# Inverting the 16x16 diagonal blocks of a triangular system by substitution on the vector engine, in a hybrid decoder layer

## The chip, the cores and the metric

The kernel runs on one core of a Trainium2 chip. Its engines are called as the profile calls them: PE is the matrix engine (PEld its weight load), DVE the vector engine (VectorE), ACT the scalar engine (ScalarE), POOL is GpSimd, SP the engine that only issues transfers. Each executes its own instructions in order; they wait for each other through semaphores. The metric is the device time of one execution in microseconds, median over runs.

## The reference

One layer of a decoder for a prompt of 256 tokens and eight samples of four tokens, model width 2048, float32. Three branches work on the same normalised input: a gated short convolution (A), a gated DeltaNet (B, 8 heads of 128) and a chunked gating MLP (C). Gates merge them, an output projection and a gated ConvFFN follow. The change touches branch B of the prompt:

```python
kb = kc * bc[..., None]
lmat = jnp.where(strict, jnp.einsum('nbhcd,nbhed->nbhce', kb, kc) * decay, 0.0)
eye = jnp.eye(C, dtype=jnp.float32)
tmat = lax.linalg.triangular_solve(eye + lmat, jnp.broadcast_to(eye, lmat.shape),
                                   left_side=True, lower=True, unit_diagonal=True)
u = jnp.einsum('nbhce,nbhef->nbhcf', tmat, vb)
w = jnp.einsum('nbhce,nbhed->nbhcd', tmat, kb * jnp.exp(gcum)[..., None])
```

For every head and every chunk of tokens a unit lower triangular matrix I + L is inverted. The result does not depend on the chunk length; the kernel takes chunks of 128 tokens, so it inverts 16 matrices of 128x128 (8 heads, 2 chunks).

## The kernel before

**The stream.** All large weights come as 614 tiles of 128 x 8 x 128 (`raw`, 512 KB, four buffers, issued from SP). ACT rounds a tile to `wh` (L74), DVE forms the remainder `wl = raw - wh` (L81), each with three buffers, and PE multiplies the eight 128x128 blocks of the tile with the 288 token columns in three passes: wh times the activations' high part (L202), wh times their low part (L203), wl times the high part (L204). A unit of 16 or 8 such blocks accumulates in one `acc` bank of PSUM and is then evacuated. One tile of the stream, 24 matmuls, is called a slot here. At the start of a slot `Stream.next` emits, in this order: one background step, outstanding `wl`, the load of the tile five ahead, `wh` and `wl` of the tile two ahead, and the evacuations that were put off.

**The background.** Everything else that needs PE between units is written as a generator, `delta()`, whose `yield`s cut it into steps; `pump` takes one step at the start of a slot. Beside the units for q, k and v it takes one step in every second slot: when a unit of these has just ended, `heavy` skips the step. The order of every engine's queue is the order in which the code emits. So a step's instruction that waits holds up what that engine was given later: on DVE the next `wl`, on PE the next slot's matmuls.

**The solve.** `delta()` goes through four groups g of two heads, four matrices (head, chunk) each, tiles [128, 4, 128]. It normalises k, forms k k^T and k q^T (L750, L751), scales k k^T into L in place (`dec`, four L119), and inverts by doubling: at level s the blocks of size s on the diagonal are joined in pairs. `T` holds the inverse so far and `U` its transpose; `B` is L times a mask m_s that leaves the squares to be eliminated at this level. At s=1 one product with the identity (L761) turns B; then for s = 2, 4, ..., 64, in two steps:

- first step: PE forms four products w of B and U (L771), ACT copies them to `W`, POOL masks the next B (L778);
- second step: PE forms four products of T and W (L782) and four of W and T (L784), DVE subtracts them from U and T.

One correction (L790, L799) and the rest of the recurrence follow. In the profile `bank` is a PSUM bank of the background and `mall` holds the masks; `U1`, `vn`, `on`, `sq` are tiles [128, 4, 128] that later parts use. Of the four groups, g=0 runs beside the q, k, v units (about 190 to 350 us), g=1 and g=2 beside the gate and output units of branch C, and g=2's end and g=3 beside branch A, whose units have a short convolution.

Of the kernel before, what the change touches and what calls it, by code (L numbers as in the profile page):

```python
# [6 lines left out]
F32 = mybir.dt.float32  # L7
F32R = mybir.dt.float32r
AF = mybir.ActivationFunctionType
ALU = mybir.AluOpType  # L10
AX = mybir.AxisListType

P = 128
# [19 lines left out]

V_LNI, V_LN1, V_LN2, V_CA, V_CB, V_CF, V_NB = 0, 32, 64, 96, 120, 216, 345
V_N = 346
MK = ("tri", "mbT", "mbS", "m1", "m2", "m4", "m8", "m16", "m32", "m64",
      "tri4", "ones4", "mbT4", "mbS4", "ones")
SM_HM, SM_BM, SM_N = 0, 4, 12

# [59 lines left out]
def body(tc, I, O):  # L99
    nc = tc.nc  # L100
    V, A, G, PE = nc.vector, nc.scalar, nc.gpsimd, nc.tensor
    top = ExitStack()

    def pool(stack, name, bufs=1, psum=False):
        if psum:
            return stack.enter_context(tc.tile_pool(name=name, bufs=bufs, space=bass.MemoryType.PSUM))
        return stack.enter_context(tc.tile_pool(name=name, bufs=bufs))

    def copy(out, in_, scale=None):
        if scale is None:  # L110
            A.activation(out=out, in_=in_, func=AF.Copy)  # L111
        else:
            A.activation(out=out, in_=in_, func=AF.Identity, scale=scale)

    def tt(out, a, b, op):
        V.tensor_tensor(out=out, in0=a, in1=b, op=op)  # L116

    def stt(out, a, s, b, op0, op1):
        V.scalar_tensor_tensor(out=out, in0=a, scalar=s, in1=b, op0=op0, op1=op1)  # L119
# [13 lines left out]
    def mid(ap, n):  # L133
        return ap.unsqueeze(1).to_broadcast([ap.shape[0], n, ap.shape[1]])
# [8 lines left out]
    tmp = pool(top, "tmp", 2)  # L143
# [5 lines left out]
    def bank():  # L149
        return bgp.tile([P, 512], F32, name="bank", tag="bank")  # L150
# [82 lines left out]
    ident = const.tile([P, P], F32, name="ident")  # L233
# [142 lines left out]
        copy(e[:, r:r + NTP], a[:, 0:NTP])  # L376
        copy(es[:, :, r:r + LS], samp(a[:, NTP:NT]))

    # ---------------------------------------------------------------- input norm
    mstack = ExitStack()  # L380
    Mp = pool(mstack, "Mp")
    M = Mp.tile([P, KD, NT], F32, name="M")
# [10 lines left out]
    for j in range(2):  # L393
        s = BLK[j][0]
# [27 lines left out]
    st.subs()  # L422
    st.dma(4)

    # ---------------------------------------------------------------- branch C
    wsT = cp.tile([P, H, P], F32, name="wsT")
    wsS = cp.tile([NTS, H, NTS], F32, name="wsS")
    bsr = cp.tile([P, H, P], F32, name="bsr")
# [1 line left out]
    tri = cp.tile([P, P], F32, name="trim")  # L430
# [8 lines left out]
    G.dma_start(out=gbr, in_=I["lnc"])  # L439
    G.dma_start(out=tri, in_=I["masks"][:, 1 + MK.index("tri"), :])  # L440
    G.dma_start(out=tri4, in_=I["masks"][0:NTS, 1 + MK.index("tri4"), 0:NTS])
    G.dma_start(out=wsT, in_=I["wsT"])
# [91 lines left out]
    flush()  # L534
    cstack.close()

    # ---------------------------------------------------------------- branches A, B
    astack = ExitStack()
    ap = pool(astack, "ap")
    QF = ap.tile([P, H, NTP], F32, name="QF")  # L540
# [99 lines left out]
    def delta():  # L640
        ds = ExitStack()
        mp = pool(ds, "dmask")
        mk = {}
        mall = mp.tile([P, len(MK), P], F32, name="mall")
        G.dma_start(out=mall, in_=I["masks"][:, 1:1 + len(MK), :])
        for i, n in enumerate(MK):
            mk[n] = mall[:, i, :]
# [6 lines left out]
        KF, VF = (kvp.tile([P, H, NTP], F32, name=n) for n in ("KF", "VF"))  # L654
        QKV.extend((KF, VF))
        ddp = ds.enter_context(tc.tile_pool(name="ddp", bufs=1, space=bass.MemoryType.DRAM))
        identR = mp.tile([P, P], F32R, name="identR")
        copy(identR, ident)
        yield
        ps = bank()  # L660
        gp = bg_g[:, 0:2, 8:16]
# [3 lines left out]
        f = lambda i: dtok[:, i].rearrange("p c h -> p (c h)")  # L665
# [16 lines left out]
        def D(tag, dt=F32, n=4):  # L682
            return dp.tile([P, n, P], dt, name=tag, tag=tag)

        def b4(bk):
            return bk[:, :].rearrange("p (u t) -> p u t", t=P)

        I4 = mid(ident, 4)
# [11 lines left out]
        for g in range(4):  # L700
# [20 lines left out]
            sq = D("sq")  # L721
# [9 lines left out]
            dT = D("decT")  # L731
# [16 lines left out]
            kk, kq = b4(bank()), b4(bank())  # L748
# [3 lines left out]
            for u in range(4):  # L752
                hh, c = divmod(u, 2)
                stt(Dm[:, u, :], kk[:, u, :], bg_g[:, c, 2 * g + hh:2 * g + hh + 1], Dm[:, u, :], ALU.mult, ALU.mult)
            L = Dm
            B = D("B", F32R)
            tt(B, L, mid(mk["m1"], 4), ALU.mult)
            yield
            w = b4(bank())
            for u in range(4):  # L760
                PE.matmul(w[:, u, :], lhsT=B[:, u, :], rhs=identR, start=True, stop=True)  # L761
            U, T = D("U", F32R), D("T", F32R)
            tt(T, I4, B.bitcast(F32), ALU.subtract)
            tt(U, I4, w, ALU.subtract)
            B = D("B", F32R)
            G.tensor_tensor(out=B, in0=L, in1=mid(mk["m2"], 4), op=ALU.mult)
            yield
            for s in (2, 4, 8, 16, 32, 64):
                w = b4(bank())
                for u in range(4):  # L770
                    PE.matmul(w[:, u, :], lhsT=B[:, u, :], rhs=U[:, u, :], start=True, stop=True)  # L771
                W = D("W", F32R)
                copy(W, w)
                if s == 2:
                    tt(dT, kq, dT, ALU.mult)
                if s < 64:
                    B = D("B", F32R)
                    G.tensor_tensor(out=B, in0=L, in1=mid(mk["m%d" % (2 * s)], 4), op=ALU.mult)  # L778
                yield
                pu, pt = b4(bank()), b4(bank())  # L780
                for u in range(4):
                    PE.matmul(pu[:, u, :], lhsT=T[:, u, :], rhs=W[:, u, :], start=True, stop=True)  # L782
                for u in range(4):
                    PE.matmul(pt[:, u, :], lhsT=W[:, u, :], rhs=T[:, u, :], start=True, stop=True)  # L784
                tt(U, U.bitcast(F32), pu, ALU.subtract)
                tt(T, T.bitcast(F32), pt, ALU.subtract)
                yield
            w = b4(bank())
            for u in range(4):
                PE.matmul(w[:, u, :], lhsT=L[:, u, :], rhs=U[:, u, :].bitcast(F32), start=True, stop=True)  # L790
            F0, F = D("sq"), D("W", F32R)
# [5 lines left out]
            w = b4(bank())  # L797
            for u in range(4):
                PE.matmul(w[:, u, :], lhsT=T[:, u, :], rhs=F[:, u, :], start=True, stop=True)  # L799
            U1 = D("U1")  # L800
            tt(U1, U.bitcast(F32), w, ALU.add)
            yield
            vn, on = D("vn"), D("on")
            S = D("S", n=2)
            for c in range(2):
                us = (c, 2 + c)
                if c:
                    w = b4(bank())
# [8 lines left out]
                w = b4(bank())  # L817
# [4 lines left out]
                w = b4(bank())  # L822
# [15 lines left out]
            sq = D("sq")  # L838
# [20 lines left out]
        mp = pool(ds, "smask")  # L859
# [34 lines left out]
        def E(tag, n=1):  # L894
            return dp.tile([P, n * P], F32, name=tag, tag=tag)

        for p in range(2):
# [4 lines left out]
            Dm, dT = E("sdec"), E("sdecT")  # L902
# [9 lines left out]
            sq = E("ssq", 2)  # L912
# [22 lines left out]
            B = E("sB")  # L935
# [5 lines left out]
            for hl in range(4):  # L941
                for b in range(NB):
                    PE.matmul(kso[:, :, hl, b, :], lhsT=stt_[4 * p + hl][:, b, :], rhs=KQv[:, :, hl, b, :], start=True, stop=True)  # L943
                if hl == 0:
                    w = bank()
                    PE.transpose(w[:, 0:P], B, ident)
                    U, T, B2 = E("sU"), E("sT"), E("sB2")
# [3 lines left out]
                if hl == 1:  # L951
                    w = bank()
# [3 lines left out]
                if hl == 2:  # L956
                    w = bank()
# [7 lines left out]
            w = bank()  # L965
            for i in range(2):
                PE.transpose(w[:, i * P:(i + 1) * P], KS[:, i * P:(i + 1) * P], ident)
            on = E("son")
# [3 lines left out]
            w = bank()  # L972
            PE.matmul(w[:, 0:P], lhsT=U, rhs=R, start=True, stop=True)
            copy(kv[:, P:2 * P], w[:, 0:P])
            vn = kv[:, P:2 * P]
# [6 lines left out]
            w = bank()  # L982
# [52 lines left out]
        ds.close()  # L1035

    background[0] = delta()
    next(background[0])

# [94 lines left out]
        unit("win", (C_G + 2048, m), X, KD, gate_evac(gs))  # L1134
        unit("wb", m, YB, H, out_b(m))

    # ---------------------------------------------------------------- output projection, LN1
    l1stack = ExitStack()
    l1p = pool(l1stack, "l1p")
    Y = l1p.tile([P, KD, NT], F32, name="Y")  # L1140
# [147 lines left out]
            chain[m]()  # L1288
    flush()

    # ---------------------------------------------------------------- gated embedding, ConvFFN
    def pg_evac(m):
        def e(a):
            s = held()
            A.activation(out=s, in_=a[:, 0:NT], func=AF.Sigmoid)

            def fin():
                tt(M[:, m, :], M[:, m, :], s, ALU.mult)
                t = short()
                tt(t, XH[:, m, :].bitcast(F32), XL[:, m, :].bitcast(F32), ALU.add)  # L1300
                stt(M[:, m, :], t, ALPHA, M[:, m, :], ALU.mult, ALU.add)
            staged.append(fin)
        return e
# [48 lines left out]
    for half, nf in enumerate(FH):  # L1352
        for i in range(nf):
            f = f0 + i
# [11 lines left out]
    op = pool(fstack, "op")  # L1366
# [36 lines left out]
def _masks(np):  # L1403
    i = np.arange(P)
    r, c = i[:, None], i[None, :]
    blk = (r // 4) == (c // 4)
    f = np.float32
    m = [(r == c).astype(f), (r <= c).astype(f),
         np.where(c >= r, f(0), f(-BIG)).astype(f), np.where(r > c, f(0), f(BIG)).astype(f)]
    for s in (1, 2, 4, 8, 16, 32, 64):  # L1410
        m.append((((r // (2 * s)) == (c // (2 * s))) & ((r // s) % 2 == 1) & ((c // s) % 2 == 0)).astype(f))
    m += [((r <= c) & blk).astype(f), blk.astype(f),
          np.where((c >= r) & blk, f(0), f(-BIG)).astype(f), np.where((r > c) & blk, f(0), f(BIG)).astype(f),
          np.ones((P, P), f)]
    return np.ascontiguousarray(np.stack(m, 1))
# [88 lines left out]
```

## Time and profile before

| | us |
|---|---|
| median of 3 runs | 2128.73 |
| lowest and highest run | 2127.16, 2128.85 |
| span of the profiled execution | 2130.0 |
| PE busy | 2118.1 |
| DVE busy | 1201.7 |
| ACT busy | 963.9 |
| POOL busy | 240.6 |

The profiled execution is known by its span, from its first to its last instruction, 2130.0 us; it lies 1.3 us above the median of the runs. Busy shares are means over stages. In rows of the chain of waits and of the timeline the first number is the start in the span, the second the duration, both in us; a bracket gives the idle time ahead of the instruction on its engine and what ended it. In rows of groups stand the busy time in us, the mean of one in ns, and the idle time before. In rows of DMA issues the last number is the median time from issue to landing in us. In rows of windows stand, after the length, busy time and count for PE, PEld, DVE, ACT and POOL, then the granted clock of PE as a share of full speed, the DMA share and GB/s.

### The profile page before, as it was taken

Reading aid. Unit: us, or ns where it says so; the run is one execution under the profiler, and the core shown is the slowest. Engines: PE = TensorE matmul, PEld = TensorE weight load, DVE = VectorE, ACT = ScalarE, POOL = GpSimd, SP = SyncE. Lnnn points to the kernel's source line nnn. Section 1 sums busy time; section 2 is a strip of 40 time slices with the busy share of each in tenths; the row PEclk is TensorE's granted clock in tenths of the full one; section 3 lists DMA queues with packets and bytes.
Section 4 is the critical chain, followed back from the end, with each engine's and each line's share of the span. In section 5 each row is a group of like instructions: output and inputs, shape, how many; then the busy total and the mean of one; then the engine's idle time right before and its main releaser. Section 6 shows DMA issues by size and latency. Waiting matters only on the chain.

```text
span 2130.0 us, 38253 instructions
## 1 busy us (share of the span) xinstructions
PE 2118.1 (99%) x15866; PEld 2095.6 (98%) x15866; DVE 1201.7 (56%) x1640; ACT 963.9 (45%) x1484; POOL 240.6 (11%) x447
## 2 busy tenths in 40 slices
PE   9999999999999999999999999999999999999999
PEld 7999999999999999999999999999999999999997
DVE  5657765555665556555577755555544455555444
ACT  6447554343434445443344634444433344444333
POOL 1112320101111212000000201111100011111000
PEclk9999999999999999999999999999999999999998
DMA  6444444443435456444544444444444444444442
GB/s 232 146 160 155 158 154 147 141 145 138 147 138 188 144 212 215 163 168 163 184 166 143 154 168 165 162 168 162 165 168 163 164 168 161 167 166 169 162 157 93
DMA packets 95998, 345.66 MB, mean 162 GB/s; under 512 B 11072, under 2 KB 11632, under 8 KB 95664
## 3 DMA queue, kind: packets, MB, share of 16 engines
q1 hardware_dynamic: 92352, 331.11, 44.5%
q0 software_dynamic: 3472, 12.11, 1.8%
q8 instruction: 124, 2.03, 0.4%
q14 instruction: 50, 0.41, 0.1%
HBM read 334.90 MB, written 8.28 MB: 161 GB/s over the span
## 4 chain that ended last, share of the span: by engine, by line
PE 98%; DVE 1%; ACT 0%; DMA 0%; issue 0%; POOL 0%; POOLq 0%; SPq 0%; DVEq 0%; ACTq 0%
PE acc L202 31%; PE acc L204 31%; PE acc L203 30%; PE bank L310 1%; PE bank L943 1%; PE bank L784 1%; PE bank L782 0%; PE bank L771 0%; PE bank L276 0%; DMA yt<-in_x 0%; PE bank L718 0%; DVE lnst L268 0%; PE bank L1022 0%; PE bank L825 0%; PE bank L751 0%; PE bank L790 0%
## 5 line engine op out<-in xcount | busy, mean ns | idle before, releaser
L81 DVE TENSOR_TENSOR wl<-raw,wh 128x1024 fp32r<-128x1024 f32 x612 | 757.9, 1239 | 747.8 <-ACT wh L74 747.5
L202 PE MATMUL acc<-XH,wh 128*128 128x288 f32 x3536 | 1056.5, 299 | 0.0
L203 PE MATMUL acc<-XL,wh 128*128 128x288 f32 x3536 | 1043.8, 295 | 0.8 <-DVE XL L116 0.8
L204 PE MATMUL acc<-XH,wl 128*128 128x288 f32 x3536 | 1040.7, 294 | 0.0
L74 ACT ACTIVATE wh<-raw 128x1024 fp32r<-128x1024 f32 x612 | 646.5, 1058 | 714.3 <-PE acc L203 582.1
L204 PEld LDWEIGHTS acc<-XH,wl 128*128 128x128 f32 x3536 | 666.4, 188 | 0.0
L203 PEld LDWEIGHTS acc<-XL,wh 128*128 128x128 f32 x3536 | 665.1, 188 | 1.2 <-DVE XL L116 1.0
L202 PEld LDWEIGHTS acc<-XH,wh 128*128 128x128 f32 x3536 | 663.9, 188 | 1.5
L204 PE MATMUL acc<-HH,wl 128*128 128x288 f32 x688 | 204.6, 297 | 0.0
L202 PE MATMUL acc<-HH,wh 128*128 128x288 f32 x688 | 204.5, 297 | 0.0
L203 PE MATMUL acc<-HL,wh 128*128 128x288 f32 x688 | 203.6, 296 | 0.0
L203 PEld LDWEIGHTS acc<-HL,wh 128*128 128x128 f32 x688 | 129.8, 189 | 0.0
L202 PEld LDWEIGHTS acc<-HH,wh 128*128 128x128 f32 x688 | 129.5, 188 | 0.2
L204 PEld LDWEIGHTS acc<-HH,wl 128*128 128x128 f32 x688 | 129.2, 188 | 0.0
L360 POOL COPY nhf<-ext 128x2 f32<-128x2 f32 x43 | 41.7, 971 | 704.6 <-ACT ext L111 704.6
L202 PE MATMUL acc<-YH,wh 128*128 128x288 f32 x384 | 115.3, 300 | 0.0
L203 PE MATMUL acc<-YL,wh 128*128 128x288 f32 x384 | 113.2, 295 | 0.0
L204 PE MATMUL acc<-YH,wl 128*128 128x288 f32 x384 | 112.9, 294 | 0.0
L119 DVE SCALAR_TENSOR_TENSOR cvo<-ext,cvec,cvo 128x304 f32<-128x304 f32 (+1 forms) x174 | 93.3, 536 | 12.0 <-ACT cvo L366 8.4
L202 PE MATMUL acc<-MH,wh 128*128 128x288 f32 x256 | 76.2, 298 | 0.0
L203 PE MATMUL acc<-ML,wh 128*128 128x288 f32 x256 | 75.5, 295 | 0.0
L204 PE MATMUL acc<-MH,wl 128*128 128x288 f32 x256 | 75.3, 294 | 0.0
(388 smaller groups left out, 1747.2 us busy)
## 6 DMA issues: line engine op xcount, KB each, us to landing
raw<-in_wall SPq DMA_DIRECT2D x612, 512.0 KB, 3.2
st<-in_sd POOLq DMA_DIRECT2D x8, 512.0 KB, 7.3
out_nds<-st SPq DMA_DIRECT2D x8, 512.0 KB, 2.9
yt<-in_x SPq DMA_DIRECT2D x9, 256.0 KB, 5.9
out_y<-vo SPq DMA_DIRECT2D x7, 288.0 KB, 2.1
gbr<-in_lnc POOLq DMA_DIRECT2D x1, 1024.0 KB, 6.2
dec<-gd POOLq DMA_DIRECT2D x8, 128.0 KB, 4.3
M<-in_wall SPq DMA_DIRECT2D x2, 512.0 KB, 5.1
```

What stands on the lines that cost most here:

```text
L74: self.nc.scalar.activation(out=h, in_=r, func=AF.Copy)
L81: self.nc.vector.tensor_tensor(out=l, in0=r, in1=h.bitcast(F32), op=ALU.subtract)
L119: V.scalar_tensor_tensor(out=out, in0=a, scalar=s, in1=b, op0=op0, op1=op1)
L202: PE.matmul(o, lhsT=wh, rhs=xh, start=start, stop=False)
L203: PE.matmul(o, lhsT=wh, rhs=xl, start=False, stop=False)
L204: PE.matmul(o, lhsT=wl, rhs=xh, start=False, stop=stop)
L310: PE.transpose(ps[:, s:s + w], self.yt[0:w, j, k * P:(k + 1) * P], ident[0:w, 0:w])
L360: G.tensor_copy(out=dst[:, 0:r], in_=e[:, NTP:NTP + r])
L784: PE.matmul(pt[:, u, :], lhsT=W[:, u, :], rhs=T[:, u, :], start=True, stop=True)
L943: PE.matmul(kso[:, :, hl, b, :], lhsT=stt_[4 * p + hl][:, b, :], rhs=KQv[:, :, hl, b, :], start=True, stop=True)
```

## The change

The levels s = 1, 2, 4 and 8 go. In their place the eight 16x16 diagonal blocks of each of the four matrices, 32 blocks, are brought onto 32 partitions, one block each, and inverted there by forward substitution:

- DVE multiplies L by a mask of the diagonal blocks and by -1 and reduces it over the eight column blocks, so that each of the 128 rows holds its 16 columns for four matrices: `cmp`, 128 x 64. POOL writes this to DRAM (`cd`).
- POOL loads it back in four transfers as `Lb`, 32 partitions of 16x16 (in the tile `vn`), and sets `T16` (in the tile `on`) to the identity.
- For i = 1 to 15 DVE multiplies the first i rows of the inverse by row i of Lb and reduces, which gives row i of the inverse: two operations, on i x i columns and 32 partitions. Yields stand after i = 5, 9 and 12.
- A copy appends the transpose; POOL writes both to DRAM (`td`) and loads them back in eight transfers of 128 pieces of 64 bytes (`ex`, in the tile `U1`).
- DVE makes T and POOL makes U by spreading `ex` over the diagonal blocks with the mask. POOL then makes B for level 16. Levels 16, 32 and 64 are as before.

Eight yields go and eight come. The names A to I are used in the prediction for the steps from the products k k^T on: A ends with the write of `cd`, B loads `Lb`, C to F substitute (F ends with the write of `td`), G loads `ex`, H makes T, U and B, I is the first step of level 16.

```diff
-        identR = mp.tile([P, P], F32R, name="identR")
-        copy(identR, ident)
...
             L = Dm
+            bd4 = mid(mk["bd16"], 4)
+            tmp = D("sq")
+            stt(tmp, L, -1.0, bd4, ALU.mult, ALU.mult)
+            cmp = D("U1").rearrange("p u t -> p (u t)")[:, 0:64]
+            V.tensor_reduce(out=cmp.rearrange("p (u j) -> p u j", j=16),
+                            in_=tmp.rearrange("p u (r j) -> p u j r", j=16), axis=AX.X, op=ALU.add)
+            cd = ddp.tile([P, 64], F32, name="cd", tag="cd", bufs=2)
+            G.dma_start(out=cd, in_=cmp)
+            tt(dT, kq, dT, ALU.mult)
+            yield
+            Lb = D("vn")[0:32].rearrange("p u t -> p (u t)")[:, 0:256].rearrange("p (i j) -> p i j", j=16)
+            for u in range(4):
+                G.dma_start(out=Lb[8 * u:8 * u + 8], in_=cd[:, 16 * u:16 * u + 16].rearrange("(r i) j -> r i j", i=16))
+            T16 = D("on")[0:32].rearrange("p u t -> p (u t)")
+            G.memset(T16[:, 0:256], 0.0)
+            G.memset(T16[:, 0:256:17], 1.0)
+            TB = T16[:, 0:256].rearrange("p (i c) -> p i c", c=16)
+            yield
+            pr = D("sq")[0:32].rearrange("p u t -> p (u t)")
+            for i in range(1, 16):
+                q = pr[:, 0:i * i].rearrange("p (c j) -> p c j", j=i)
+                tt(q, TB[:, 0:i, 0:i].rearrange("p j c -> p c j"), mid(Lb[:, i, 0:i], i), ALU.mult)
+                V.tensor_reduce(out=TB[:, i, 0:i], in_=q, axis=AX.X, op=ALU.add)
+                if i in (5, 9, 12):
+                    yield
+            V.tensor_copy(out=T16[:, 256:512].rearrange("p (c i) -> p c i", i=16), in_=TB.rearrange("p i c -> p c i"))
+            td = ddp.tile([32, 512], F32, name="td", tag="td", bufs=2)
+            G.dma_start(out=td, in_=T16)
+            yield
+            ex = D("U1").rearrange("p u t -> p (u t)")[:, 0:128].rearrange("p (m u c) -> p m u c", m=2, u=4)
+            for u in range(4):
+                for m in range(2):
+                    G.dma_start(out=ex[:, m, u, :], in_=td[8 * u:8 * u + 8, 256 * m:256 * m + 256].rearrange("r (i c) -> r i c", c=16))
+            yield
+            U, T = D("U", F32R), D("T", F32R)
+            for m, X2 in enumerate((T, U)):
+                (V, G)[m].tensor_tensor(out=X2.rearrange("p u (r c) -> p u r c", c=16),
+                                        in0=ex[:, m].unsqueeze(2).to_broadcast([P, 4, 8, 16]),
+                                        in1=bd4.rearrange("p u (r c) -> p u r c", c=16), op=ALU.mult)
             B = D("B", F32R)
-            tt(B, L, mid(mk["m1"], 4), ALU.mult)
-            yield
-            w = b4(bank())
-            for u in range(4):
-                PE.matmul(w[:, u, :], lhsT=B[:, u, :], rhs=identR, start=True, stop=True)
-            U, T = D("U", F32R), D("T", F32R)
-            tt(T, I4, B.bitcast(F32), ALU.subtract)
-            tt(U, I4, w, ALU.subtract)
-            B = D("B", F32R)
-            G.tensor_tensor(out=B, in0=L, in1=mid(mk["m2"], 4), op=ALU.mult)
+            G.tensor_tensor(out=B, in0=L, in1=mid(mk["m16"], 4), op=ALU.mult)
             yield
-            for s in (2, 4, 8, 16, 32, 64):
+            for s in (16, 32, 64):
...
-                if s == 2:
-                    tt(dT, kq, dT, ALU.mult)
```

**POOL in group g=1, before.** `so` and `rr` are row factors, computed ahead of the solve; then only the six products B:

```order
L131 TENSOR_TENSOR so<-so,mhalf 128x4
L130 TENSOR_SCALAR rr<-ss 128x8
L131 TENSOR_TENSOR rr<-rr,mhalf 128x8
L766 TENSOR_TENSOR B<-dec,mall 128x512
L778 TENSOR_TENSOR B<-dec,mall 128x512 x5
L694 DMA dec<-gd 128x2x128 x2
```

The same place after the change; `U_4247` and `U_4484` are tiles U1, `vn` holds Lb and `on` T16, L790 is the product U:

```order
L131 TENSOR_TENSOR rr<-rr,mhalf 128x8
L761 DMA cd<-U_4247 128x64
L766 DMA vn<-cd 8x16x16 x4
L768 MEMSET on 32x256
L769 MEMSET on 32x16
L781 DMA td<-on 32x512
L786 DMA U_4484<-td 128x1x16 x8
L790 TENSOR_TENSOR U<-U_4484,mall 128x512
L794 TENSOR_TENSOR B<-dec,mall 128x512
L804 TENSOR_TENSOR B<-dec,mall 128x512 x2
L692 DMA dec<-gd 128x2x128 x2
```

Three products have gone; fourteen transfers stand now between the kk scaling and the first product that level 16 needs, and U and B stand behind them.

**DVE in group g=1, before**, from the kk scaling (`dec`) into level 2:

```order
L119 SCALAR_TENSOR_TENSOR dec<-bank,bg_g,dec 128x128 x4
L116 TENSOR_TENSOR B<-dec,mall 128x512
L81 TENSOR_TENSOR wl<-raw,wh 128x1024
L116 TENSOR_TENSOR M<-acc,u 128x288
L116 TENSOR_TENSOR T<-ident,B 128x512
L116 TENSOR_TENSOR U<-ident,bank 128x512
L81 TENSOR_TENSOR wl<-raw,wh 128x1024
L116 TENSOR_TENSOR decT<-bank,decT 128x512
```

After, the same stretch as far as the first operations of step C, and the end of step F up to T:

```order
L119 SCALAR_TENSOR_TENSOR dec<-bank,bg_g,dec 128x128 x4
L119 SCALAR_TENSOR_TENSOR sq<-dec,mall 128x512
L758 TENSOR_REDUCE U_4247<-sq 128x64
L116 TENSOR_TENSOR decT<-bank,decT 128x512
L81 TENSOR_TENSOR wl<-raw,wh 128x1024
L116 TENSOR_TENSOR M<-acc,u 128x288
L81 TENSOR_TENSOR wl<-raw,wh 128x1024
L116 TENSOR_TENSOR sq<-on,vn 32x1
L776 TENSOR_REDUCE on<-sq 32x1
```

```order
L116 TENSOR_TENSOR sq<-on,vn 32x225
L776 TENSOR_REDUCE on<-sq 32x15
L779 COPY on<-on 32x256
L81 TENSOR_TENSOR wl<-raw,wh 128x1024 x2
L116 TENSOR_TENSOR M<-acc,u 128x288
L790 TENSOR_TENSOR T<-U_4484,mall 128x512
L81 TENSOR_TENSOR wl<-raw,wh 128x1024 x2
```

Two operations of 512 columns now lead to the first write, the 31 small ones of C to F stand between the `wl` of four slots, and T, which reads `ex`, stands ahead of the `wl` of the next slots. On PE the four products of level 16 (L799 after the change) stand behind the same slot of the stream as before, with no background product between k q^T and them.

More of the change, by code (lines that the diff above doesn't have):

```diff
@@ L35 @@
 V_N = 346
-MK = ("tri", "mbT", "mbS", "m1", "m2", "m4", "m8", "m16", "m32", "m64",
+MK = ("tri", "mbT", "mbS", "m1", "m2", "bd16", "m16", "m32", "m64",
       "tri4", "ones4", "mbT4", "mbS4", "ones")
@@ L1409, in _masks @@
          np.where(c >= r, f(0), f(-BIG)).astype(f), np.where(r > c, f(0), f(BIG)).astype(f)]
-    for s in (1, 2, 4, 8, 16, 32, 64):
+    for s in (1, 2, 0, 16, 32, 64):
+        if not s:
+            m.append(((r // 16) == (c // 16)).astype(f))
+            continue
         m.append((((r // (2 * s)) == (c // (2 * s))) & ((r // s) % 2 == 1) & ((c // s) % 2 == 0)).astype(f))
```

## The prediction

> **What bounds the kernel now.** I read the page first: busy time, then the chain that ended last. Its rows:
>
> ```profile
> PE 2118.1 (99%) x15866; PEld 2095.6 (98%) x15866; DVE 1201.7 (56%) x1640; ACT 963.9 (45%) x1484; POOL 240.6 (11%) x447
> ...
> PE 98%; DVE 1%; ACT 0%; DMA 0%; issue 0%; POOL 0%; POOLq 0%; SPq 0%; DVEq 0%; ACTq 0%
> ```
>
> The matrix engine is the chain almost throughout, so a matmul that vanishes is time saved, and any wait put in front of a matmul is time lost. Next I read the chain in order of time over head group g=1 (start, duration, what), where one background step goes with each slot of 24 streamed matmuls:
>
> ```profile
> 227.97 0.40 PE bank L761 x4
> 234.80 0.39 PE bank L771 x4
> ...
> 277.12 0.39 PE bank L771 x4
> ...
> 369.81 0.39 PE bank L761 x4
> 373.44 0.39 PE bank L771 x4
> 377.07 0.39 PE bank L782 x4
> 377.46 0.45 PE bank L784 x4
> ...
> 388.85 0.39 PE bank L771 x4
> 396.56 0.39 PE bank L771 x4
> ```
>
> The L771 rows of g=1 are the levels s=2, (4), 8, 16. A level takes two slots and 7.71 us, of which its own twelve matmuls are 0.39 + 0.39 + 0.45 = 1.23; the rest is two slots of weights, 3.2 us each. Call the steps A (the kk products), B, C, ... I (level 16): in before I starts at 396.56. In g=0 (the rows at 227.97, 234.80, 277.12), which runs beside the convolution units, a step comes in every second slot only, 6.8 us apart.
>
> **What is removed.** Per group four products with the identity and 36 of levels 2, 4 and 8: 0.39 + 3 x 1.23 = 4.1 us on PE. If all else hides, four groups save 16.4 us. The eight yields removed are eight yields added, so level 16 stands at the same slot as before; removed alone, I would start at 396.56 - 4.1 = 392.4 in g=1. With them go three copies of W on ScalarE, the products B of the small levels on GpSimd and nine operations of 512 columns on VectorE a group, the copy of the identity and one mask plane: all beside PE's stream, so worth nothing of their own. The product decT moves up behind the reduction in A, where it delays one wl by 0.6 us that has more than a slot in hand.
>
> **What is added** is a chain that no slot of 3.2 us covers. Its prices are in these rows (start, duration, instruction, idle before and its releaser; then groups and DMA issues with us to landing):
>
> ```profile
> 170.29 0.18 DVE L116 TENSOR_TENSOR pp<-pp,z 128x24 f32<-128x24 f32 x1
> 170.50 0.18 DVE L124 TENSOR_SCALAR pp<-pp 128x24 f32<-128x24 f32 x1
> ...
> 201.43 0.69 DVE L116 TENSOR_TENSOR decT<-dec,mall 128x512 f32<-128x512 f32 x1
> 202.16 0.69 DVE L116 TENSOR_TENSOR dec<-dec,mall 128x512 f32<-128x512 f32 x1
> ...
> 366.43 1.12 DVE L119 SCALAR_TENSOR_TENSOR dec<-bank,bg_g,dec 128x128 f32<-128x128 f32 x4 [1.96 <-PE bank L750]
> ...
> 378.70 1.22 DVE L81 TENSOR_TENSOR wl<-raw,wh 128x1024 fp32r<-128x1024 f32 x1
> 379.83 0.45 DVE L116 TENSOR_TENSOR M<-acc,u 128x288 f32<-128x288 f32 x1
> ```
> ```profile
> 187.19 0.51 POOL L678 DMA_DIRECT2D gd<-gT  x1
> 190.52 1.48 POOL L694 DMA_DIRECT2D dec<-gd  x2 [2.83 <-DMA gd<-gT]
> ...
> 725.71 1.67 POOL L980 DMA_DIRECT2D kv<-kvd  x3 [2.36 <-DMA kvd<-skv]
> ```
> ```profile
> L766 POOL TENSOR_TENSOR B<-dec,mall 128x512 fp32r<-128x512 f32 x4 | 5.2, 1291 | 38.5 <-PE bank L761 38.5
> ```
> ```profile
> dec<-gd POOLq DMA_DIRECT2D x8, 128.0 KB, 4.3
> ...
> kv<-kvd POOLq DMA_DIRECT2D x6, 128.0 KB, 3.1
> ...
> out_ndp<-S POOLq DMA_DIRECT2D x4, 128.0 KB, 2.4
> ...
> out_y<-vo SPq DMA_DIRECT2D x2, 144.0 KB, 1.7
> ...
> hv<-in_hv POOLq DMA_DIRECT2D x1, 8.0 KB, 3.3
> ```
>
> Dependent vector operations start 0.21 us apart at 24 columns and 0.73 at 512: 0.19 us plus 1.04 ns a column. A weight remainder (wl) holds the queue 1.13 us (378.70 to 379.83). A write to DRAM and the load that needs it are 190.52 - 187.19 = 3.3 us apart on GpSimd's queue. Loads of 128 pieces go out every 1.67 / 3 = 0.56 us. For the landing of a load I take 3.1 us: hv, 128 pieces of 64 bytes, is the same shape (3.3), kv the same queue behind the same kind of write. The bounds are 2.4 (the fastest of this queue) and 4.3 (dec, two at once).
>
> The chain in g=1, from the end of the kk scaling on VectorE, 366.43 + 1.12 = 367.55:
> - scaling by the block mask and the reduction, 512 columns each: 1.4; to 369.0.
> - cd written, loads can go: 3.3; the fourth load goes out 3 x 0.56 = 1.7 later and lands 3.1 after: 377.1. Step C should begin at 373.0, so VectorE stands four us, with the next wl behind it.
> - C to F, 30 small operations in pairs over i x i columns (1,240 columns for each kind): 30 x 0.19 + 2 x 1.3 = 8.3, and the copy 0.45 (as 256 columns): 8.7 in all. Between them stand three wl (3.4) and one M (0.4): 12.5; to 389.6.
> - td written: 3.3; 392.9. The eighth load 7 x 0.56 = 3.9 later: 396.8; landed 399.9.
> - U and then B on GpSimd, 1.29 each (L766), in one queue: 402.4.
>
> Level 16 starts at 402.4 where it started at 396.56: 5.9 us late, 10.0 later than with the removal alone. PE waits in slot I for about 8.7 us; about 1 us more is already lost before, since wl for slot E comes at 380.3 and PE wants it at 379.7, and for slots G and H some tenths. GpSimd's other work of this stretch (conv tails in g=3) is 0.4 us a unit and falls into the 3.3 us after td. In g=2 and g=3 the slots carry a similar load on VectorE (g=3: YL and two products in place of M), so I take 5.9 for each.
>
> In g=0 a step has two slots: F's end to the end of B is 3.3 + 3.9 + 3.1 + 2.6 = 12.9, and F's own 2.9 go ahead of it; from F to I are three steps, 20.5: hidden, saving 4.1. GpSimd's loads go ahead of a convolution's ext there, 4.5 us in a pair of slots of 6.8; I cost that at nothing, and if that cover is gone it is at most those 4.5 us once or twice.
>
> **A long wait of PE also lowers its clock.** In these rows from the start of the kernel (first: start, duration, PE matmuls; then windows with PE's busy time and the granted clock):
>
> ```profile
> 6.66 3.40 PE L245 MATMUL bank<-wz 128*128 128x512 bf16 x15
> 12.40 0.33 PE L310 MATMUL bank<-ident,yt 128*128 128x128 f32 x1 [2.34 <-DVE yt L126]
> 13.55 2.75 PE L310 MATMUL bank<-ident,yt 128*128 128x128 f32 x11 [0.82 <-DVE yt L126]
> ...
> 17.12 0.44 PE L202 MATMUL acc<-XH,wh 128*128 128x288 f32 x1
> 17.36 0.44 PE L203 MATMUL acc<-XL,wh 128*128 128x288 f32 x1
> ...
> 22.20 0.29 PE L202 MATMUL acc<-XH,wh 128*128 128x288 f32 x1
> 22.33 0.29 PE L203 MATMUL acc<-XL,wh 128*128 128x288 f32 x1
> ```
> ```profile
> 14.00:15.00 1.00, 0.98 (x6) 0.60 (x5) 1.00 (x2) 0.92 (x3) 1.00 (x3) 1.00 1.00 410
> 15.00:16.00 1.00, 1.00 (x6) 0.47 (x4) 1.00 (x3) 0.97 (x3) 1.00 (x3) 0.55 1.03 419
> ...
> 21.00:22.00 1.00, 1.00 (x6) 1.00 (x6) 1.00 (x3) 0.26 (x1) 0.00 (x0) 0.54 1.05 407
> ```
>
> PE was nearly idle from 10.06 to 13.55; the clock fell to half at about 15.45, 5.4 us after the last dense matmul, and came back at 21.95. Streamed matmuls stood 0.24 us apart at half and 0.13 at full clock. Mine is a wait of 8.7 us. If the low stretch starts 5.4 us in and lasts 6.5, 3.2 us of it fall on work, and 45% of that, 1.4 us, is lost; if all 6.5 fall on work, 2.9. I take 2.2 a group.
>
> [...]
>
> **Sum.** g=0: -4.1. g=1 to 3: 3 x (5.9 + 2.2) = 24.3. Together +20.2 us. The profiled span is 2130.0, 1.3 above the median of the runs (2128.73); laid on the median: 2148.9, so 2149.
>
> **The rivals.** A time within 0.2% of before (4.3 us) counts as the same.
> - *All hidden, faster:* 2128.7 - 16.4 = 2112.3. It needs B and U by 392.4 in g=1 to 3, ten us earlier than in my sum; the run is faster than noise as soon as the lateness, with what the clock takes, is under zero. For it speaks that the eight steps are kept apart by yields. Against it: the four transfer legs alone are 12.8 us, and even at 1.7 (the shortest landing in the table, of another queue) they would shrink by some 6 us, not ten. Chance 0.08.
> - *Shorter legs, no difference:* landings of 2.4 take 0.6 or 0.7 off each leg, 2.6 a group; small operations at 0.12 in place of 0.19 take 2.1. Then lateness is 1.2, and with 1.4 for the clock 3 x 2.6 - 4.1 = +3.7: 2132. Both must hold. Chance 0.12.
> - *The eight loads pile up, much slower.* Of dec, the slowest took 5.5:
> ```profile
> DMA to landing us min/median/max: 3.4/4.3/5.5
> ```
>   64-byte pieces by the thousand may do as badly; with 5.5 us (2.4 more) at two legs a group is 4.8 later, and with 2.9 for the clock 3 x (10.7 + 2.9) - 4.1 = +36.7: 2165. Chance 0.15.
> - My forecast has 0.65, with a range of its own of 2134 (clock not lowered: +13.6 is 2142; landings of 2.4 as well: +5.8) to 2158 (landings of 4.3 at both load legs, the clock's full 2.9: 3 x (8.3 + 2.9) - 4.1 = +29.5).
>
> [...]
>
> **How the numbers follow.** 2149 is the likeliest case. The range goes from 2130, inside the second rival, to 2166, past the third's value; outside are the hidden case (0.08), half of the second rival and the tail of the third, some 0.2 in all. Faster: 0.08. Same: 0.09, most of the second rival. Slower: 0.83.
>
> **What would show it.** In the new trace the L799 matmuls of level 16 should, in g=1, 2 and 3, stand some 35 us behind the end of the kk scaling, with PE idle 8 to 10 us ahead of them and released by GpSimd's B; in g=0 not. T on VectorE should wait for a DMA onto the ex columns. The granted clock should dip to half for some us after each of three waits. GpSimd's first Lb and ex loads should each wait some 2.4 us for the write. I am wrong if C to F take far less than 12.5 us (the step of 0.19 an operation), if the legs are far from 3.1 to 3.3, or if the wait is found at wl instead.

## The result, and the profile after

The changed kernel takes 2151.76 us, median of four runs (2150.6 to 2154.36), against 2128.74 before: 1.0112 times as long, with a 95% interval of 1.01 to 1.0124. It is 1.1% slower; the prediction was 2149. The profiled execution of it took 2150.6 us, with a span of 2148.8.

The first rows of the page, busy time and the chain that ended last:

```profile
PE 2107.9 (98%) x15706; PEld 2083.7 (97%) x15706; DVE 1221.1 (57%) x1740; ACT 957.9 (45%) x1471; POOL 268.9 (13%) x503
...
PE 93%; issue 3%; POOL 1%; DMA 1%; DVE 1%; ACT 0%; SPq 0%; POOLq 0%; DVEq 0%; ACTq 0%
```

PE has 160 matmuls less (4 x 40) and 10 us less of busy time, and yet its share of the chain fell from 98% to 93%. What took the place is a chain through GpSimd, DMA and VectorE. The time lies in three of the four head groups. Each begins with twelve transposes of k, q and v; here are these rows of the chain in order of time, before, with the first row behind group 3:

```profile
192.45 1.31 PE bank L718 x12
...
350.29 1.31 PE bank L718 x12
...
456.93 1.31 PE bank L718 x12
...
563.57 1.31 PE bank L718 x12
...
666.57 0.44 PE bank L854 x4
```

and after:

```profile
192.43 1.31 PE bank L716 x12
...
345.92 1.31 PE bank L716 x12
...
460.86 1.31 PE bank L716 x12
...
576.54 1.31 PE bank L716 x12
...
688.69 0.44 PE bank L880 x4
```

The differences from row to row: g=0 153.49 in place of 157.84, 4.35 us shorter; g=1 114.94 for 106.64, g=2 115.68 for 106.64, g=3 112.15 for 103.00: 8.30, 9.04 and 9.15 longer. The sum is +22.1. The spans differ by 18.8 only, because the profiled execution of before ran its last transposes at half clock (granted clock 0.50 from 2118 us on, 1.00 in the changed kernel's). These 3.0 us lie behind everything that the change touches:

```profile
2115.11 10.85 PE bank L310 x43
```
```profile
2137.23 7.86 PE bank L310 x43
```

(before, then after, the same 43 transposes in the chain.) So 22.1 on the median of before is 2150.9, and the profiled run of after took 2150.6.

What ended PE's waits, after (us in total, times, longest):

```profile
PE bank L799 <- POOL B L794: 24.2, 3, 8.1
PE acc L204 <- DVE wl L81: 5.5, 6, 1.3
```

Three waits of 8.1 us at level 16, in g=1, 2 and 3, and six small ones at the remainder of the weights. The chain of g=1 shows step by step what PE waited for:

```profile
362.06 1.14 DVE dec L119 x4
...
363.94 1.05 DVE U L758
...
365.28 1.81 DMA cd<-U
...
367.75 1.87 POOL vn L766 x3
...
370.71 15.61 issue
386.34 1.90 DMA td<-on
...
388.52 4.07 POOL U L786 x7
392.59 1.98 DMA U<-td
...
394.64 2.31 POOL U L790
396.94 1.23 POOL B L794
...
398.22 1.12 PE bank L799 x4
...
408.20 0.39 PE bank L799 x4
```

The `issue` of 15.61 us is the rest of the landing and VectorE's substitution: the view put none of its operations there, but the timeline has them from 373.18 to 385.78, and the write of td follows 0.56 us later. From the end of the kk scaling (363.18) to the first product of level 16 (398.22) it is 35.0 us.

### The profile page after: what moved, and what is told of

Same layout as the page of the kernel before. It is cut to its first block, busy times and chain, and to the rows that moved or that the text cites. A ratio compares the mean times of both kernels' runs of the same rounds, so it can differ in the third digit from the quotient of the medians.

```text
span 2148.8 us, 38077 instructions
## 1 busy us (share of the span) xinstructions
PE 2107.9 (98%) x15706; PEld 2083.7 (97%) x15706; DVE 1221.1 (57%) x1740; ACT 957.9 (45%) x1471; POOL 268.9 (13%) x503
## 4 chain that ended last, share of the span: by engine, by line
PE 93%; issue 3%; POOL 1%; DMA 1%; DVE 1%; ACT 0%; SPq 0%; POOLq 0%; DVEq 0%; ACTq 0%
PE acc L202 30%; PE acc L204 29%; PE acc L203 29%; PE bank L310 1%; PE bank L969 1%; POOL U L786 1%; PE bank L276 0%; DMA yt<-in_x 0%; PE bank L799 0%; DMA U<-td 0%; POOL U L790 0%; DMA td<-on 0%; POOL vn L766 0%; DMA cd<-U 0%; PE bank L810 0%
## 5 line engine op out<-in xcount | busy, mean ns | idle before, releaser
L119 DVE SCALAR_TENSOR_TENSOR cvo<-ext,cvec,cvo 128x304 f32<-128x304 f32 (+1 forms) x174 | 95.2, 547 | 13.9 <-ACT cvo L366 10.4
```

## The experiments

Two theories stood against each other: that the *latency of the serial chain* against the eight slots that cover it sets the loss, with the clock's drop on top, or that the substitution as such, or one of its parts alone, is to blame. Each kernel is the changed kernel with one edit, if nothing else is said.

**The levels taken out, nothing in their place.** Steps A to H keep their yields, T and U are the identity times the block mask, so the output differs: the 16x16 blocks are not inverted.

```diff
-            ...     # mask product, reduction, cd, Lb, substitution, td and ex, with their yields
+            for _ in range(7):
+                yield
...
-                in0=ex[:, m]...
+                (V, G)[m].tensor_tensor(out=X2, in0=I4, in1=bd4, op=ALU.mult)
```

> Levels 1 to 8 are left out and nothing takes their place: T and U start as the identity, so the output is not the reference's. The eight yields stay. Theory: each group gains what group 0 gained in the changed kernel, 4.4 us: 2128.7 - 17.5 = 2111.3. Rival: the removed matmuls are partly beside the stream and the gain is smaller, 2115 to 2125.

2111.95 us, 0.9919 times before (0.9905 to 0.9934), 16.8 less. What the removal gives if all else hides is thus measured, and agrees with 16.4. The substitution and what hangs on it costs the difference to 2151.76: 39.8 us.

**PE kept busy through the wait.** 33 zero matmuls go ahead of level 16 in g=1 to 3; level 16 itself waits as before.

```diff
+            if g:
+                warm(33)
             for s in (16, 32, 64):
```

> The changed kernel with 33 matmuls on zeros (128x512, about 7.5 us) put on PE ahead of level 16 in groups 1 to 3, where PE waits 8.1 us anyway. The work is not needed for the result. Theory, clock: PE is not idle any more, the granted clock stays at 1.00 and the 2.2 to 2.4 us a group that the half clock costs come back: about 2144.5 (2142 to 2147). Rival: the wait alone is the loss, the clock costs nothing: 2151.8, or more by what the matmuls overshoot.

2147.99 us, 1.009 (1.0073 to 1.0107). The chain's rows of its first two levels in g=1:

```profile
398.04 0.66 PE bank L801 x4
406.03 0.39 PE bank L801 x4
```

Level 16 starts as far behind the transposes of the group as in the changed kernel (52.24 for 52.30 us), and yet level 32 follows 7.99 us behind it, where in the changed kernel it is 408.20 - 398.22 = 9.98. In g=2 and g=3 the changed kernel has 10.29 and 10.54, this one 7.99 and 7.98. These 2.0 to 2.6 us, 6.9 in three groups, are what the lowered clock takes from the work behind the wait. The profiled run of this kernel, 2144.4, shows nearly all of it (-6.2 against the profiled run of the changed kernel); its three other runs, 2147.7 to 2148.7, had a mean granted clock of 0.996 or 0.997 for 0.998, and where they lost it no trace tells. So the median gives 3.8, one us short of the range expected, and the size between 3.8 and 6.9 stays open.

**Fewer transfers.** One Lb load and one ex load in place of four and eight; `cd` and `td` are laid out so that the Lb load has one piece a partition and the ex load four pieces of 128 bytes.

```diff
-            for u in range(4):
-                G.dma_start(out=Lb[8 * u:8 * u + 8], in_=cd[...])
+            G.dma_start(out=Lf, in_=cd.rearrange("u (r i) j -> (u r) (i j)", i=16))
...
-            for u in range(4):
-                for m in range(2):
-                    G.dma_start(out=ex[:, m, u, :], in_=td[...])
+            G.dma_start(out=exf.rearrange("p (u x) -> p u x", x=32), in_=td.rearrange("u p x -> p u x"))
```

> The changed kernel with one transfer in place of four for Lb and one in place of eight for ex (the layout in DRAM is turned so that the pieces are the same number or fewer: 512 of 64 bytes written for cd, 512 of 128 bytes read for ex). Theory, issues: 3 x 0.6 and 7 x 0.63 us of issuing leave the chain, a few tenths come back for the larger transfers; the chain is about 30 us, the wait about 3, the clock perhaps still lowered: 2128 to 2136. Rival, pieces: the small pieces are what takes the time, and they are as many: about 2151.8, or within 3 us of it.

2141.11 us, 1.0056 (1.0041 to 1.0071): 10.7 better than the change, but short of the 2128 to 2136 expected. GpSimd's timeline at the end of the chain in g=1 (start, duration, instruction, idle before and what ended it):

```profile
387.70 0.80 POOL L786 DMA_DIRECT2D U<-td  x1 [1.71 <-DMA td<-on]
391.81 1.75 POOL L790 TENSOR_TENSOR U<-U,mall 128x512 fp32r<-128x512 f32 x1 [3.30 <-DMA U<-td]
393.52 2.24 POOL L794 TENSOR_TENSOR B<-dec,mall 128x512 fp32r<-128x512 f32 x1
```

The seven issues saved (4.07 us) come back in part: from the load's issue to U it is 4.1 us, where in the changed kernel it was 6.1 (388.52 to 394.64). The single load of 64 KB needs longer than the last of eight did, and the products behind it cost 4.0 instead of 3.6. The longest wait fell from 8.1 to 6.5 us. The low clock cost as much as before: from level 16 to level 32 it is 9.75, 9.91 and 10.81 us in the three groups, 1.8 to 2.8 over the 7.98 of the kernel with zero matmuls.

**The products off the end of the chain.** U goes to VectorE behind T, and level 16's B to GpSimd ahead of the substitution.

```diff
+            B = D("B", F32R)
+            G.tensor_tensor(out=B, in0=L, in1=mid(mk["m16"], 4), op=ALU.mult)
             T16 = ...
...
-                (V, G)[m].tensor_tensor(...
+                V.tensor_tensor(...
-            B = D("B", F32R)
-            G.tensor_tensor(out=B, in0=L, in1=mid(mk["m16"], 4), op=ALU.mult)
```

> The changed kernel with the product U on DVE behind T, and the first B on GpSimd ahead of the substitution, so that nothing of GpSimd stands behind the last load. Theory, latency: the end of the chain shrinks from U and B on GpSimd (3.5 us from the landing, measured) to one product on DVE (0.6 to 0.7): 2.8 us a group in three groups, 2151.8 - 8.4 = 2143.4 (2141 to 2146). Rival, work: DVE has one product more and is the engine that holds back wl; 2151 to 2154.

2142.51 us, 1.0066 (1.0049 to 1.0083), as expected; the longest wait is now for U on VectorE:

```profile
PE bank L799 <- DVE U L792: 17.3, 3, 6.3
```

**More slots.** Two yields more behind the ex loads in g=1 to 3, so that two more slots of weights run before level 16 is due.

```diff
             yield
+            for _ in range(2 if g >= 1 else 0):
+                yield
             U, T = ...
```

> The changed kernel with two more yields behind step G in groups 1 to 3, so that ten steps and not eight lie between the kk scaling and level 16. Theory, latency: the chain of 35 us from the scaling to B is fixed, and the stream now has 6.4 us more to run under it; PE's wait in slot I falls from 8.1 to about 1.7 us and the clock no longer drops, a group loses about 0.1 in place of 8.8 us, group 0 still gains 4.4: about 2124.6 (2122 to 2128). Rival, work: the added instructions on DVE and POOL hold back wl whatever the steps; more steps change nothing: about 2151.8.

2135.19 us, 1.003 (1.0017 to 1.0043): 16.6 better than the change, 10.6 worse than expected. PE still waits (the first row). The two others are the product U of g=1 on GpSimd's timeline with the idle time ahead of it, in this kernel and then in the changed one:

```profile
PE bank L801 <- POOL B L796: 10.5, 3, 4.0
```
```profile
397.12 2.31 POOL L792 TENSOR_TENSOR U<-U,mall 128x512 fp32r<-128x512 f32 x1 [3.75 <-DMA U<-td]
```
```profile
394.64 2.31 POOL L790 TENSOR_TENSOR U<-U,mall 128x512 fp32r<-128x512 f32 x1 [1.38 <-DMA U<-td]
```

The same eight loads, issued at nearly the same time (the last one done at 393.37 and 393.26), hold up U for 3.75 us in place of 1.38. In the changed kernel PE stood still and the weight stream with it, so the loads had the DMA engines nearly to themselves; with two more slots they run beside it. The windows of that microsecond (busy time by engine, granted clock, DMA share, GB/s), first the changed kernel, then this one:

```profile
393.00:394.00 1.00, 0.00 (x0) 0.00 (x0) 0.00 (x0) 0.00 (x0) 0.26 (x1) 0.50 0.12 13
```
```profile
393.00:394.00 1.00, 1.00 (x10) 1.00 (x9) 0.00 (x0) 0.62 (x1) 0.37 (x1) 1.00 1.10 372
```

The waits are 4.03, 2.67 and 3.78 us, so two slots, 6.5 us, bought only 4.0 to 5.4 us of each: it seems that part of the old landing time had been cheap because PE was waiting. And these shorter waits still lowered the clock: level 32 comes 10.2, 9.5 and 10.4 us behind level 16, some 6 us over 3 x 7.98, which the expectation had put at nothing.

**A shorter substitution.** It stops after row 5, so the output differs; the yields stay.

```diff
             for i in range(1, 16):
+                if i > 5:
+                    if i in (9, 12):
+                        yield
+                    continue
```

> The changed kernel with the substitution stopped after row 5 (10 of 30 small operations; rows 6 to 15 are left out, so the output is not the reference's), all yields, transfers and products kept. Theory, the small operations are a serial part of the chain: 6.7 us less of it, PE's wait falls from 8.1 to about 1.4 us and the clock is not lowered: 3 x 8.5 less, 2126 (2123 to 2131). Rival, the transfers set the end and the small operations lie beside them: 2148 to 2152.

2138.1 us, 1.0047 (1.0032 to 1.0062), between the two expectations and in neither. In g=1 the write of td goes out 6.3 us earlier (380.02 for 386.34), but the loads follow only 4.4 us earlier:

```profile
380.02 0.53 POOL L785 DMA_DIRECT2D td<-on  x1 [9.24 <-issue]
384.14 4.73 POOL L790 DMA_DIRECT2D U<-td  x8 [3.59 <-DMA td<-on]
```

The write held GpSimd 3.59 us in place of 1.65 (2.90 and 1.75 in g=2 and g=3). As with the loads above, the DMA engines were fuller: shares of 0.88 to 0.96 in the windows from 381 to 384 us here, of 0.06 and 0.32 in the two from 386 to 388 in the changed kernel. And the waits, now 4.55 to 4.94 us, still lowered the clock, whose cost did not shrink with them. Level 16 and level 32 of g=1 and g=2:

```profile
393.94 1.12 PE bank L803 x4
404.65 0.39 PE bank L803 x4
...
505.53 0.91 PE bank L803 x4
515.04 0.39 PE bank L803 x4
```

10.71 and 9.51 us apart: 2.7 and 1.5 over the 7.98 of the kernel with zero matmuls. The granted clock stood at half for 6.8 us in g=1 and for 3.4 in g=2, 5.9 and 3.4 of it on work, while in g=1 of the changed kernel 5.8 of the 10.2 us at half clock were over before PE went on.

**All of it together.** The fewer transfers and the moved products, and one yield more behind the Lb load and one behind the ex load (g=1 to 3):

```diff
             yield                                   # behind the Lb load
+            for _ in range(1 if g >= 1 else 0):
+                yield
...
             yield                                   # behind the ex load
+            for _ in range(1 if g >= 1 else 0):
+                yield
```

> The single transfers of the second run, the products of the fifth, and two more yields in groups 1 to 3, one between the load of Lb and the substitution and one between the load of ex and the products. Theory, latency: the chain is 32.9 - 2.8 = 30.1 us and ten slots give 31; PE does not wait at level 16, and DVE no longer stands for Lb with wl behind it: within 3 us of the kernel without the levels, 2112 to 2116. Rival, work: 30 operations and the products still cost the stream their time on DVE, some 8 us a group: 2130 or more.

2112.55 us, 0.9928 (0.9913 to 0.9943): faster than both kernels. What is left of PE's wait:

```profile
PE bank L803 <- DVE U L796: 0.8, 1, 0.8
```

The clock was at full throughout g=1 to 3. The same kernel once more, in five rounds:

> The sixth run's kernel once more, in five rounds beside the kernel before, for the size of its gain. Expected as there: 2112.5 (2111 to 2115), 0.7 to 0.8% under the kernel before; the rival is chance in the sixth run: over 2118.

2112.25 us, 0.9924 (0.9912 to 0.9937), 0.3 us from the kernel without the levels (2111.95); by the ratios, each to the kernel before measured beside it, the two are 1 us apart.

**Without the yields, and without the fewer transfers.** The first kernel is the version with all of it less its two yields, the second less its fused transfers (four and eight loads again).

> The sixth run without its two extra yields: single transfers and products on DVE, eight steps. Theory, latency: the chain is 30.0 us against 24.9 us of slots; PE waits some 3.8 us a group at level 16 and one at wl, and the clock falls for one or two windows of 3.4 us: 2129 to 2134, so nearly the whole gain over the sixth run (2112.6) is the cover of two slots. Rival, the shorter chain alone does it and the yields matter little: 2112 to 2118.

2130.91 us, 1.0014 (1.0005 to 1.0023), as expected: the two yields are worth 18.4 us here.

> As the sixth run, but with the twelve loads of the changed kernel. Theory, latency: the chain is 35 - 2.8 = 32.2 and, since the loads land later while the weight stream runs (3.6 us behind the last issue in the first run against 2.0), 33.8; ten slots give 31, so PE waits up to 2.8 us a group and the clock stays: 2116 to 2122. Rival: with both yields the number of transfers does not matter and it equals the sixth run within 1 us.

2132.73 us, 1.0022 (1.0013 to 1.0032): both expectations missed by more than ten us. The three waits as the timeline of PE has them:

```profile
396.95 0.63 PE L803 MATMUL bank<-U,B 128*128 128x128 f32 x4 [3.15 <-DVE U L796]
...
509.99 1.08 PE L803 MATMUL bank<-U,B 128*128 128x128 f32 x4 [4.10 <-DVE U L796]
...
628.33 1.09 PE L803 MATMUL bank<-U,B 128*128 128x128 f32 x4 [4.39 <-DVE U L796]
```

The waits, 11.6 us, and behind two of them the low clock (the first product takes 1.1 us in place of 0.63) (2.2 and 2.7 us from level 16 to 32 beyond 7.98) make up most of the 20.2 us between this kernel and the one with single loads. That the low clock has its share was tried by itself: the same kernel with 14 zero matmuls ahead of level 16.

```diff
+            if g:
+                warm(14)
             for s in (16, 32, 64):
```

> The seventh run with 14 matmuls on zeros (about 3.2 us, not needed for the result) on PE ahead of level 16 in groups 1 to 3, where PE waits 3.2 to 4.4 us. Theory, clock: such short waits already lower the clock (13.6 us at half in the seventh run's trace), which costs 5 us over the three groups beside the wait itself; they come back: 2125.5 to 2129 against 2132.7. Rival: the clock costs nothing at waits as short as this: 2132 to 2134.

2125.14 us, 0.9985 (0.9976 to 0.9994): 7.6 less than without them. That is more than the 4.9 that the profiled run of the kernel without them shows, which was the shortest of its ten (2130.99); the profiled run of this kernel was the longest of its ten (2127.99). In its trace level 32 follows 7.95 or 7.96 us behind level 16 in each group.

## Why the prediction was right, and where it was off

The mechanism was right: the chain is longer than its eight slots in g=1 to 3, PE waits at level 16 until GpSimd's B is done, the clock falls at each of the three waits, and in g=0 all is hidden. Some sizes were not.

- *Removal.* Right: 16.8 measured by the kernel without the levels, 16.4 predicted; g=0 alone 4.35 for 4.1.
- *The chain.* 35.0 us for 34.9, but with errors that cancel, so the closeness is luck. By the prediction's own sign of being wrong (legs far from 3.1 to 3.3) three of its four transfer legs were wrong, predicted 0.8 to 1.1 us too long. To the write of cd 2.1 for 1.4 (the reduction over a strided view took 1.04 for 0.7, and 0.3 went by from its end to the write's issue). The two writes, issue to first load, 2.5 and 2.2 for 3.3 each. Lb loads and landing 5.4 for 4.8, C to F with td's issue 13.2 for 12.5 (of this 0.56 from the copy's end to the issue, a step that the prediction did not have), seven issues 4.1 for 3.9, last landing 2.05 for 3.1, U and B 3.6 for 2.6.
- *U and B.* The step "U and then B on GpSimd, 1.29 each" was mis-sized: in g=1 U took 2.31, and B 1.26 with VectorE idle. In g=3 U took 1.25, but the remainder wl beside it took 2.30 in place of 1.22, and B then 2.24:

```profile
625.62 1.25 POOL L790 TENSOR_TENSOR U<-U,mall 128x512 fp32r<-128x512 f32 x1 [1.42 <-DMA U<-td]
```
```profile
625.66 2.30 DVE L81 TENSOR_TENSOR wl<-raw,wh 128x1024 fp32r<-128x1024 f32 x1
```

  In g=1 wl had started 0.03 us ahead of U (394.61) and took 1.22. In both, whichever started first took its usual time, and the other ended 1.1 us behind it. It looks as if the two engines held each other up; no run tried this by itself.
- *The lateness.* Level 16 stands 52.30, 52.73 and 52.59 us behind the group's transposes, where it stood at 46.27 before in each: 6.0, 6.5 and 6.3 us late for 5.9. In g=1 PE waits 8.1 us there and 1.7 before it, at two remainders wl (8.7 and about 1 predicted).
- *The clock.* 2.0 to 2.6 us from level 16 to 32 for 2.2 (bounds 1.4 to 2.9). The windows (busy time by engine, granted clock, DMA share, GB/s) show where it fell and rose:

```profile
392.00:393.00 1.00, 0.00 (x0) 0.00 (x0) 0.00 (x0) 0.00 (x0) 1.00 (x3) 0.72 0.24 20
...
402.00:403.00 1.00, 1.00 (x7) 1.00 (x6) 0.17 (x1) 0.00 (x0) 0.00 (x0) 0.66 0.00 0
```

  Half clock from 392.4 to 402.7 is 10.2 us; 4.5 of them fall on work, of which 45% is 2.0. The prediction had 5.4 us until the drop and 6.5 at half: the drop came 2.3 us after PE stopped at 390.1, and lasted longer, so the price was right and its shape wrong. (Its own window row, 0.55 for the microsecond from 15, puts the fall at 15.1 and not at 15.45: 5.0 us and 6.8, with the same 3.2 on work.)
- *The sum.* From the transposes to level 16 the three groups lost 18.8 us and behind it 7.7, together 26.5 for the predicted 24.3. Of the 2.2 more, 1.1 is lateness, 0.3 the clock, and 0.8 a term that was left out: behind a wait the first products of level 16 take 0.66 instead of 0.39 even at full clock (the kernel with zero matmuls), 0.27 in each group.
- *The rivals.* "All hidden" needs what the last version has: single loads, no product behind the landing and two more slots; then it holds to 0.3 us. "Shorter legs" had three legs right (2.5, 2.2 and 2.05), but the operations and the products cost more than predicted, not less. The loads did not pile up: the median to landing is 3.1 us for ex, 3.9 for Lb.
- *The low stretches, and the legs together.* The low stretches behind the waits came as 3.4, 6.8 and 10.2 us, as the last section shows, where the prediction took 6.5; one of 3.4 cost 1.5 us (five rows, g=2). A wait of 2.67 us was enough for a fall in one kernel and one of 3.15 not in another. From issue to landing the writes of cd and td took 1.8 and 1.9 us and the last load of ex 1.98. The four legs measured 10.3 us together for the prediction's 12.8, and the rest of the chain took 2.7 us more than its other terms.

The forecast held; several expectations behind it did not. Those of two more yields, fewer transfers, five rows and many loads missed their ranges by 5 to 11 us, each expected faster than it ran. Common to them is the clock, which they put at nothing or left open for the waits that remained, and which still took 4.9 to 6.8 us in the traces of these kernels. The one of two more yields also took the duration of the loads from a stretch in which PE and its weight stream stood still. The one of many loads did not: it allowed 3.6 us behind the last issue, and its chain of 33.8 us measured 34.2 in g=1; its waits came to 11.6 us instead of at most 8.4. That loads slow down beside the stream is seen in rows (1.38 to 3.75 us, 1.65 to 3.59, DMA shares beside them), but no run changed the weight stream alone; that it is the cause stays an inference.

## What to carry to other kernels

Where an in-order engine runs a stream and a step beside it becomes a chain of transfers and small operations, price the chain's whole latency against the slots that cover it: saved matmuls count only when the chain is inside. Then shorten its end first (one transfer in place of many, nothing computed behind the last landing) and give it slots, and expect each shortened leg to return a part, as here, where transfers took longer when the stream ran beside them (the loads of ex held up U for 3.75 us in place of 1.38). A wait of 2.3 to 8.1 us on PE cost 1.5 to 2.9 us more in lowered clock, or nothing in two cases, and within that range the price did not shrink with the wait: it went when the wait went, or when PE was kept busy through it.

## What the runs showed of the hardware

A multiply whose first operand is read over strided rows took more a column than the rows of before had shown. Of VectorE's timeline after the change, the first multiply of the substitution, its last, and the copy behind it:

```profile
373.18 0.15 DVE L116 TENSOR_TENSOR sq<-on,vn 32x1 f32<-32x1 f32 x1 [4.96 <-DMA vn<-cd]
...
384.42 0.54 DVE L116 TENSOR_TENSOR sq<-on,vn 32x225 f32<-32x225 f32 x1
...
385.41 0.37 DVE L779 COPY on<-on 32x256 f32<-32x256 f32 x1
```

The multiply goes from 0.15 us at one column to 0.54 at 225, 1.7 ns a column, where the prediction had 1.04; the reduction of the same 225 columns takes 0.38. That the strided read is the cause was not tried by itself. It is hardly the substitution's miss: the small operations cost less at the start (0.18 us from one to the next), and all 30 took 8.5 us for the 8.3 predicted. The miss is the 0.56 us between the end of the copy, 385.78, and the write's issue on GpSimd, 386.34; g=2 and g=3 have the same 0.56 and 0.57.

A low stretch of the clock was not always shorter behind a shorter wait. In the changed kernel, behind waits of 8.1 us, each of the three lasted 10.24 us; read from windows of 0.2 us they begin at 392.44, 508.50 and 624.55, 116.06 us apart, which is 34 times 3.41. With the substitution stopped after row 5 the stretch of g=1 lasted 6.8 us, behind a wait of 4.55, and that of g=2 3.4 us, behind one of 4.80. Windows of 3.41 us, a third of the 10.24, laid on the instants of these falls show how idle PE was ahead of each. In the changed kernel, between 300 and 700 us, PE stood idle for 67%, 88% and 100% of the window ahead of a fall, and for 38% or less of every other window at full clock. At half clock the clock stayed low behind windows with 34% to 100% idle and came back behind those with none. The wait of 2.67 us with two more yields (g=2) fell into one window (78% idle), and the clock fell; the one of 3.15 us with many loads (g=1) was shared by two (1.7 and 1.5 us idle, 49% and 44%), and there the clock stayed (window, its length, PE's busy time; the third number from the end is the granted clock):

```profile
514.85:518.26 3.41, 0.74 (x7) 0.51 (x6) 3.41 (x3) 0.00 (x0) 2.91 (x2) 1.00 0.42 154
518.26:521.67 3.41, 3.41 (x16) 3.41 (x16) 2.52 (x5) 1.88 (x3) 1.29 (x1) 0.50 0.41 154
```
```profile
392.05:395.46 3.41, 1.75 (x14) 1.51 (x12) 0.00 (x0) 0.00 (x0) 0.91 (x2) 1.00 0.44 156
395.46:398.87 3.41, 1.92 (x15) 1.95 (x16) 2.80 (x4) 1.25 (x2) 1.20 (x1) 1.00 0.01 2
```

The four runs of the changed kernel spread over 3.8 us, and the longer ones have the lower mean granted clock (0.991 twice, then 0.989 and 0.988). This fits low stretches of different length behind the three waits, but no trace of the longer runs shows it.
